# Down products in four passes over 16-byte granules, with the activations moved, in a one-core encoder layer

## Chip, core and metric

The kernel runs on one core of a Trainium2 chip. The metric is device time in microseconds (us) of one execution; the time before is the median of three runs. TensorE (PE) does the matmuls, and its weight loads are shown apart (PEld); VectorE (DVE), ScalarE (ACT) and GpSimd (POOL) work beside it, and SyncE (SP) issues the DMAs.

## The reference

One layer of a bidirectional encoder on 512 positions of width 1024, all in float32, with two half-step feed-forward blocks (FFN) around a mixing step:

```python
def swiglu(h, w_gate, w_up, w_down):
    return (jax.nn.silu(h @ w_gate) * (h @ w_up)) @ w_down
...
x = x + 0.5 * swiglu(rms_norm(x, ffn1_norm), ffn1_w_gate, ffn1_w_up, ffn1_w_down)
h = rms_norm(x, mix_norm)
u = h @ w_in
f_out = fourier_mixer(u[..., :o0], fnet_w, fnet_b)
a_out = gqa_attention(u[..., o0:o1], u[..., o1:o2], u[..., o2:], q_norm, k_norm)
x = x + jnp.concatenate([f_out, a_out], axis=-1) @ w_out
x = x + 0.5 * swiglu(rms_norm(x, ffn2_norm), ffn2_w_gate, ffn2_w_up, ffn2_w_down)
return rms_norm(x, final_norm)
```

The inner width of an FFN is 2752: 21 chunks of 128 and a tail of 64.

## The kernel before

**Operands in two parts.** Every float32 operand is split into a high and a low part that TensorE takes as `float32r`. A product is the sum of three matmuls: high weights with the high activation, high weights with the low one, low weights with the high one. `product` (lines 172 to 176) issues them, and these are the lines L173, L175 and L176 of the profile.

**An FFN.** `ffn` works through the chunks of the inner width in four groups (`GROUPS1`, `GROUPS2`). The first group's gate and up products run on the normalised input with all 512 positions. For the other groups `seven` computes gate and up of a chunk with seven products of half size instead of eight: line 407, where the moving operand is 256 columns of `rt` and the result goes to tiles named r, p and q. A chunk takes 84 of them: 7 products, 4 blocks of the input width, 3 parts. The second of a run of `seven` is cut into 64 and 192 columns (`parts_of`, `CUT`).

The activation of a chunk is put into a place of `at`: seven places, each 2 (high, low) x 512 columns. When a group is done, `down` multiplies its chunks with the down weights, for each of the eight blocks of 128 output channels (d), into a bank of PSUM `dn`: 512 columns, moving operand from `at`, weights from a slot of `ring`. The inner width's tail is two more matmuls per block, L487 and L488. `residual` (L528) then adds half of `dn` to x.

In the second FFN's last group the last three blocks (`LAST`) are done otherwise, in the stage `closing`: the first half of the positions in products of 256 columns (tiles `last`, with weights that begin `SKIP` elements into their slot), the second half by `by_tokens` (L519), where `at` is the weights and 384 columns of `tw` the moving operand. While the first group of an FFN runs, three places of `at` are lent as weight slots.

**Order.** In both FFNs TensorE's order is that of the code; the loads of weights and activations are put one step ahead by the loops (`prepare`, `PIECES`). The mixing stage between them follows a written order (`ORDER`); its matmuls are named mix in the profile. L998 to L1000 there have 256 columns from `ring`, L1057 256, 258 or 512 columns of `pos` and `both`, L1160 is a transpose.

**Places.** Tiles of a pool lie one behind another. `room` puts an unused tile between them, so many bytes of each partition. In the pool of the activations:

```python
room(ap, 192)
at = ap.tile([P, PLACES, 2, S], F32R, name=f"at{n_}")
room(ap, 192)
rt = ap.tile([P, 7, 2, KH, HALF], F32R, name=f"rt{n_}")
```

In the program that is built of it `at` begins at byte 119168 of a partition and `rt` at 148032; weights of the slots begin at 128 modulo 256, `at` at 128 and `rt` at 64.

Of the kernel before, what the change touches and what calls it, by code (L numbers as in the profile page):

```python
# [33 lines left out]
USES = "a11", "a12", "s1", "s2", "s4", "s3", "a22"  # L34
PIECES = (0, 2, 2, 0, 2, 1, 1)
KH = KD // 2
SKIP = 16
LAST = 3
CUT = 1, P // 2
HI_DVE = ("f0", "f1")  # L40
# [43 lines left out]
def encoder(ctx, tc, A, out):  # L84
    nc = tc.nc
# [6 lines left out]
    def room(pool, n):  # L92


        pool.tile([P, n // 4], F32, name=f"room{len(rooms)}")
        rooms.append(n)
# [6 lines left out]
    def bank(name):  # L103
        return pp.tile([P, S], F32, tag="bank", name=name)
# [40 lines left out]
    def raw_tile(src, name, n=KD):  # L145
        raw = wp.tile([P, KD, P], F32, tag="raw", name=f"raw_{name}")
        nc.sync.dma_start(out=raw[:, :n, :], in_=src)
        return raw
# [6 lines left out]
    def parts_of(n):  # L155

        return (slice(0, CUT[1]), slice(CUT[1], HALF)) if n == CUT[0] else (slice(0, HALF),)

    def weights(src, name, n=KD, raw=None, by_dma=False, skip=0):
        raw = raw or raw_tile(src, name, n)  # L160
        hi, lo = weight_slots(n, skip)
        if name in HI_DVE:
            nc.vector.tensor_copy(hi[:, :n, :], raw[:, :n, :])
        else:
            nc.scalar.copy(hi[:, :n, :], raw[:, :n, :])  # L165
        if by_dma:
            rest_by_dma(lo, hi, src)
        else:
            lows(lo[:, :n, :], raw[:, :n, :], hi[:, :n, :])
        return hi, lo  # L170

    def product(ps, whi, wlo, mhi, mlo, first, last, cut=False):
        nc.tensor.matmul(ps, whi, mhi, start=first, stop=False)  # L173
        for t in parts_of(CUT[0]) if cut else (slice(0, ps.shape[-1]),):
            nc.tensor.matmul(ps[:, t], whi, mlo[:, t], start=False, stop=False)  # L175
        nc.tensor.matmul(ps, wlo, mhi, start=False, stop=last)  # L176
# [92 lines left out]
    def ffn(norm, after, wgu, wd, wdt, groups, opening, closing):  # L269
# [4 lines left out]
        n_ = norm.n  # L274
        n_plain = len(groups[0])
        with tc.tile_pool(name=f"act{n_}", bufs=1) as ap, tc.tile_pool(name=f"sums{n_}", bufs=2) as sp:
            room(ap, 192)
            at = ap.tile([P, PLACES, 2, S], F32R, name=f"at{n_}")
            room(ap, 192)
            rt = ap.tile([P, 7, 2, KH, HALF], F32R, name=f"rt{n_}")  # L280
            wt, raws = [], {}
            free, where = list(range(PLACES)), {}
# [12 lines left out]
            def gate(c, between={}, by_dma=False):  # L295
                whi, wlo = weights(wgu[c], f"gu{n_}_{c}", by_dma=by_dma)
                ps = bank(f"gu{n_}_{c}")
                for k in range(KD):
                    between.get(k, int)()
                    product(ps, whi[:, k, :], wlo[:, k, :], hh[k], hl[k], k == 0, k == KD - 1)  # L300
                return ps
# [170 lines left out]
            def down(d, group, gi):  # L472

                js = [j for j in group if j != "t"]
                src, halves_ = wd[d][:, js[0] : js[-1] + 1, :], closing and gi == len(groups) - 1 and d >= KD - LAST
                raw = raws[d] = raw_tile(src, f"dn{n_}_{d}_{gi}", len(js))
                whi, wlo = weights(src, "", len(js), raw, skip=SKIP if halves_ else 0)
                if halves_:
                    token_weights(d, js)
                w = wt[d // 4][:, d % 4 * P : (d % 4 + 1) * P]  # L480

                def steps(ps, t):
                    for i, j in enumerate(group):
                        h, l = (at[:, where[j], o, t] for o in range(2))
                        first, last = i == 0, i == len(group) - 1
                        if j == "t":
                            nc.tensor.matmul(ps[:, t], w, h, start=first, stop=False)  # L487
                            nc.tensor.matmul(ps[:, t], w, l, start=False, stop=last)  # L488
                        else:
                            k = j - js[0]  # L490
                            cut = first and d == KD - LAST and t == slice(0, HALF)
                            product(ps[:, t], whi[:, k, :], wlo[:, k, :], h, l, first, last, cut)
                        yield

                return steps

            def token_weights(d, group):

                c = slice((d - KD + LAST) * P, (d - KD + LAST + 1) * P)
                hi, lo = (t[:, : len(group), c] for t in tw)  # L500
                raw = raws[d][:, : len(group)]
                nc.scalar.activation(hi, raw, AF.Copy, scale=0.5)
                nc.vector.scalar_tensor_tensor(
                    out=lo, in0=raw, scalar=0.5, in1=asf(hi), op0=ALU.mult, op1=ALU.subtract
                )
# [26 lines left out]
            every = slice(0, S)  # L532
            for gi, group in enumerate(groups):
                last = gi == len(groups) - 1
# [3 lines left out]
                else:  # L538
# [8 lines left out]
                    for i, c in enumerate(left):  # L547
# [6 lines left out]
                        while len(parts) * len(left) > (len(left) - 1 - i) * KH:  # L554
                            o = parts.pop(0)
# [14 lines left out]
                for d in range(KD):  # L570
# [8 lines left out]
                    ps = bank(f"dn{n_}_{d}_{gi}")  # L579
# [66 lines left out]
    cut = [0] + [4 * KD + k * S for k in (1, 2, 4, 6, 8)]  # L646
# [80 lines left out]
    with in_order():  # L727
        ffn(n0, n1, A["wgu1"], A["wd1"], A["wdt1"], GROUPS1, opening1, None)
# [3 lines left out]
    with tc.tile_pool(name="mix", bufs=1) as mp, tc.tile_pool(name="mixt", bufs=1) as mt:  # L732
# [69 lines left out]
        def project_ops(c, name):  # L802

            weight_ops(f"w{name}", A["wins"][c])

            def step(k):
                if k == 0:
                    banks[name] = bank_for(name, {"v": 1, "k": 3, "q0": 3}.get(name, 2))
                whi, wlo = ws[f"w{name}"]
                product(banks[name], whi[:, k, :], wlo[:, k, :], hh[k], hl[k], k == 0, k == KD - 1)  # L810

            for k in range(KD):
                op(f"{name}.{k}")(lambda k=k: step(k))
# [514 lines left out]
    first, rest = out[0].rearrange("p (k s) -> p k s", s=HALF), out[1].rearrange("p (c n) -> p c n", n=D)  # L1328
# [98 lines left out]
    with in_order():  # L1427
        ffn(n2, n3, A["wgu2"], A["wd2"], A["wdt2"], GROUPS2, lambda gate, column, row: [[gate(0, {KD - 1: column}), gate(1, {3: row})]], closing)
# [122 lines left out]
```

## Time and profile before

| | |
|---|---|
| time, median of 3 runs | 838.82 us (838.07 to 838.83) |
| span of the profiled execution, first to last instruction | 836.5 us |
| time of the runs beside the span | 2.3 us |
| PE busy | 829.6 us (99%) |
| DVE busy | 640.0 us (77%) |
| ACT busy | 465.3 us (56%) |
| DMA, mean | 107 GB/s |
| mean granted TensorE clock | 0.999 |

The time of the profiled execution itself wasn't recorded apart from its span; the 2.3 us are the difference between the median of the runs and the span. A group's row gives the busy time as a union of its instructions and the mean duration of one. Matmuls overlap, since each is shown until its result is out, so how fast TensorE goes is read from the distances between starts: in the timeline, or in the chain of work that ended last, where an instruction counts until the next begins.

### The profile page before, as it was taken

What the parts mean: (1) busy time and instruction counts of PE and PEld (TensorE: products, weight loads), DVE (VectorE), ACT (ScalarE), POOL (GpSimd) and SP (SyncE); (2) the same over time, 40 slices, a digit from 0 to 9 for tenths busy, and PEclk for the clock granted to TensorE, in tenths of its full rate; (3) what the DMA queues carried; (4) which work ended last, traced back from release to release, by engine and by line L of the source; (5) the groups of instructions that cost most, each with busy time, mean ns of one, the idle gap of its engine ahead of it and who ended that gap; (6) DMA issues with size and microseconds to landing.
All of it is one profiled execution on the core that took longest, in us unless ns stands there. A gap on an engine that the chain in (4) does not pass through costs nothing.

```text
span 836.5 us, 13664 instructions
## 1 busy us (share of the span) xinstructions
PE 829.6 (99%) x5406; PEld 751.5 (90%) x5406; DVE 640.0 (77%) x1005; ACT 465.3 (56%) x778; POOL 30.7 (4%) x34
## 2 busy tenths in 40 slices
PE   9999999999999999999999999999999999999997
PEld 6888998899989998888998888899988999899986
DVE  7898896489746947699998488999954896479573
ACT  7763664167524645677786356656622673257462
POOL 0110000000000000221100000100000000000001
PEclk9999999999999999999999999999999999999999
DMA  7664322323242213532020224443232332322222
GB/s 254 171 149 161 129 89 76 120 101 139 76 138 95 67 54 114 169 99 80 26 76 26 74 86 130 114 164 121 89 120 89 133 112 66 131 102 95 68 75 101
DMA packets 31168, 89.58 MB, mean 107 GB/s; under 512 B 3712, under 2 KB 8832, under 8 KB 31104
## 3 DMA queue, kind: packets, MB, share of 16 engines
q1 hardware_dynamic: 27776, 82.61, 29.0%
q0 software_dynamic: 2608, 5.12, 3.3%
q10 hardware_dynamic: 720, 0.98, 0.3%
q8 instruction: 42, 0.69, 0.3%
q14 instruction: 22, 0.18, 0.1%
HBM read 84.24 MB, written 2.10 MB: 103 GB/s over the span
## 4 chain that ended last, share of the span: by engine, by line
PE 98%; issue 0%; DMA 0%; DVE 0%; ACT 0%; POOLq 0%; POOL 0%; DVEq 0%
PE r L407 23%; PE q L407 11%; PE dn L175 9%; PE dn L173 9%; PE dn L176 9%; PE p L407 6%; PE mix L173 3%; PE mix L175 3%; PE mix L176 3%; PE gu L693 3%; PE gu L173 3%; PE gu L176 3%; PE gu L175 3%; PE mix L1203 2%; PE mix L1160 2%; PE mix L1134 1%
## 5 line engine op out<-in xcount | busy, mean ns | idle before, releaser
L407 PE MATMUL r<-rt,ring 128*128 128x256 f32 x1686 | 209.6, 276 | 0.0
L407 PEld LDWEIGHTS r<-rt,ring 128*128 128x128 f32 x1686 | 200.6, 188 | 0.9
L175 PE MATMUL dn<-at,ring 128*128 128x512 f32 x300 | 116.7, 389 | 0.0
L176 PE MATMUL dn<-at,ring 128*128 128x512 f32 x300 | 116.7, 389 | 0.0
L173 PE MATMUL dn<-at,ring 128*128 128x512 f32 x300 | 116.7, 389 | 0.0
L407 PE MATMUL q<-rt,ring 128*128 128x256 f32 x840 | 106.6, 276 | 0.0
L123 DVE TENSOR_TENSOR ring<-s,ring 128x1024 fp32r<-128x1024 f32 x70 | 85.5, 1221 | 24.1 <-ACT ring L366 20.8
L407 PEld LDWEIGHTS q<-rt,ring 128*128 128x128 f32 x840 | 100.4, 188 | 0.0
L528 DVE SCALAR_TENSOR_TENSOR gx<-dn,gx 128x512 f32<-128x512 f32 x61 | 41.9, 689 | 74.3 <-PE dn L176 74.3
L366 ACT CAST ring<-s 128x1024 fp32r<-128x1024 f32 x70 | 73.5, 1050 | 28.0 <-PE p L407 13.7
L165 ACT CAST ring<-raw_dn 128x768 fp32r<-128x768 f32 (+3 forms) x58 | 45.4, 786 | 76.7 <-PE dn L175 60.4
L176 PEld LDWEIGHTS dn<-at,ring 128*128 128x128 f32 x300 | 56.3, 188 | 11.8
L173 PEld LDWEIGHTS dn<-at,ring 128*128 128x128 f32 x300 | 56.3, 188 | 11.3
L175 PEld LDWEIGHTS dn<-at,ring 128*128 128x128 f32 x300 | 56.3, 188 | 11.2
L123 DVE TENSOR_TENSOR ring<-raw_dn,ring 128x768 fp32r<-128x768 f32 (+3 forms) x58 | 51.6, 892 | 5.9 <-PE r L407 4.6
L407 PE MATMUL p<-rt,ring 128*128 128x256 f32 x420 | 53.3, 276 | 0.0
L123 DVE TENSOR_TENSOR ring<-raw_g,ring 128x1024 fp32r<-128x1024 f32 x35 | 42.7, 1219 | 10.4 <-PE p L407 10.3
L407 PEld LDWEIGHTS p<-rt,ring 128*128 128x128 f32 x420 | 50.2, 188 | 0.0
L366 ACT CAST ring<-raw_g 128x1024 fp32r<-128x1024 f32 x35 | 36.8, 1053 | 13.9 <-DMA raw_g<-in_wgu 8.3
L415 ACT COPY p<-r 128x256 f32<-128x256 f32 x35 | 12.9, 370 | 49.1 <-PE r L407 48.7
L439 ACT ACTIVATE g<-g 128x512 f32<-128x512 f32 x35 | 22.2, 633 | 23.4 <-DVE g L438 23.1
L375 ACT CAST ring<-raw_u 128x512 fp32r<-128x512 f32 x35 | 21.8, 624 | 16.8 <-PE q L407 15.9
(318 smaller groups left out, 1557.1 us busy)
## 6 DMA issues: line engine op xcount, KB each, us to landing
raw_g<-in_wgu SPq DMA_DIRECT2D x35, 512.0 KB, 3.6
raw_u<-in_wgu SPq DMA_DIRECT2D x35, 512.0 KB, 4.3
raw_dn<-in_wd SPq DMA_DIRECT2D x40, 384.0 KB, 3.1
raw_gu<-in_wgu SPq DMA_DIRECT2D x12, 512.0 KB, 3.5
raw_o<-in_wo SPq DMA_DIRECT2D x8, 512.0 KB, 3.5
raw_dn<-in_wd SPq DMA_DIRECT2D x8, 448.0 KB, 3.3
raw_wq<-in_wins SPq DMA_DIRECT2D x4, 512.0 KB, 4.4
raw_f<-in_winf SPq DMA_DIRECT2D x4, 512.0 KB, 4.0
```

What stands on the lines that cost most here:

```text
L123: nc.vector.tensor_tensor(out=lo, in0=src, in1=asf(hi), op=ALU.subtract)
L165: nc.scalar.copy(hi[:, :n, :], raw[:, :n, :])
L173: nc.tensor.matmul(ps, whi, mhi, start=first, stop=False)
L175: nc.tensor.matmul(ps[:, t], whi, mlo[:, t], start=False, stop=False)
L176: nc.tensor.matmul(ps, wlo, mhi, start=False, stop=last)
L366: nc.scalar.copy(hi, src)
L375: nc.scalar.copy(hi, src)
L407: nc.tensor.matmul(ps[:, t], a[:, ks], b[:, i, t], start=first and i == 0 and o == 0, stop=i == KH - 1 and o == 2, skip_group_check=not first,
L439: nc.scalar.activation(b["g"], b["g"], AF.Silu)
L528: nc.vector.scalar_tensor_tensor(out=x[d][:, t], in0=ps[:, t], scalar=0.5, in1=x[d][:, t], op0=ALU.mult, op1=ALU.add)
L693: nc.tensor.matmul(pss[c], w[:, k % 2, c], m[k], start=k == 0 and m is hh and w is hi, stop=k == KD - 1 and w is lo,)
L1160: nc.tensor.transpose(pts[n][:, c * P : (c + 1) * P], prob[t, b, c][:, kc * P : (kc + 1) * P], ident)
```

## The change

A down product whose result covers all 512 positions reads its moving operand and writes its result through `turned`: 512 columns are seen as 32 x 4 x 4 and walked with the middle factor outermost. Four passes, each of 32 granules of 4 neighbouring elements (16 bytes), 64 bytes apart. Operand and result are walked alike, so that each element lands where it did. Both tail matmuls of a block do the same. The 256-column products of `closing`, and all other products, keep their order. The filler ahead of `at` goes from 192 to 144 bytes and that behind it from 192 to 240. `SKIP` goes from 16 to 4 elements.

```diff
-SKIP = 16
+SKIP = 4
...
-    def product(ps, whi, wlo, mhi, mlo, first, last, cut=False):
+    def turned(ap):
+        return ap.rearrange("p (a b c) -> p b a c", b=4, c=4)
+
+    def product(ps, whi, wlo, mhi, mlo, first, last, cut=False, turn=False):
+        if turn:
+            ps, mhi, mlo = turned(ps), turned(mhi), turned(mlo)
+            for a, b in ((whi, mhi), (whi, mlo), (wlo, mhi)):
+                nc.tensor.matmul(ps, a, b, start=first and b is mhi and a is whi, stop=last and a is wlo)
+            return
         nc.tensor.matmul(ps, whi, mhi, start=first, stop=False)
...
-            room(ap, 192)
+            room(ap, 144)
             at = ap.tile([P, PLACES, 2, S], F32R, name=f"at{n_}")
-            room(ap, 192)
+            room(ap, 240)
             rt = ap.tile([P, 7, 2, KH, HALF], F32R, name=f"rt{n_}")
...
+                        turn = t == every
                         if j == "t":
-                            nc.tensor.matmul(ps[:, t], w, h, start=first, stop=False)
-                            nc.tensor.matmul(ps[:, t], w, l, start=False, stop=last)
+                            o, h, l = (turned(p) if turn else p for p in (ps[:, t], h, l))
+                            nc.tensor.matmul(o, w, h, start=first, stop=False)
+                            nc.tensor.matmul(o, w, l, start=False, stop=last)
                         else:
                             k = j - js[0]
                             cut = first and d == KD - LAST and t == slice(0, HALF)
-                            product(ps[:, t], whi[:, k, :], wlo[:, k, :], h, l, first, last, cut)
+                            product(ps[:, t], whi[:, k, :], wlo[:, k, :], h, l, first, last, cut, turn)
```

In the program built of the changed kernel `at` begins at byte 119136 and `rt` at 148064.

## The prediction

> **What bounds the kernel now.** I read the page first: its busy times, its granted clock, its chain, its costliest groups.
>
> ```profile
> span 836.5 us, 13664 instructions
> PE 829.6 (99%) x5406; PEld 751.5 (90%) x5406; DVE 640.0 (77%) x1005; ACT 465.3 (56%) x778; POOL 30.7 (4%) x34
> PEclk9999999999999999999999999999999999999999
> PE 98%; issue 0%; DMA 0%; DVE 0%; ACT 0%; POOLq 0%; POOL 0%; DVEq 0%
> L407 PE MATMUL r<-rt,ring 128*128 128x256 f32 x1686 | 209.6, 276 | 0.0
> L175 PE MATMUL dn<-at,ring 128*128 128x512 f32 x300 | 116.7, 389 | 0.0
> L176 PE MATMUL dn<-at,ring 128*128 128x512 f32 x300 | 116.7, 389 | 0.0
> L173 PE MATMUL dn<-at,ring 128*128 128x512 f32 x300 | 116.7, 389 | 0.0
> L407 PE MATMUL q<-rt,ring 128*128 128x256 f32 x840 | 106.6, 276 | 0.0
> L407 PE MATMUL p<-rt,ring 128*128 128x256 f32 x420 | 53.3, 276 | 0.0
> ```
>
> TensorE is 98% of the chain that ended last, at full granted clock, with nothing idle before these groups. So the time is a count of matmuls times their spacing, and any change of spacing goes straight into the end. The mean durations (389, 276 ns) overlap and are no spacing; starts are. The timeline gives them for a run of down products:
>
> ```profile
> 131.65 0.39 PE L173 MATMUL dn<-at,ring 128*128 128x512 f32 x1
> ...
> 135.51 0.39 PE L176 MATMUL dn<-at,ring 128*128 128x512 f32 x1
> ```
>
> Eighteen rows, seventeen intervals: 3.86 / 17 = 227 ns for 512 columns. The chain, where matmuls follow without a gap, gives the other widths:
>
> ```profile
> 82.85 2.72 PE r L407 x24
> 436.71 1.44 PE mix L1057 x12
> 820.95 1.57 PE last L519 x9
> ```
>
> That is 113.3 ns (256 columns), 120 ns (258) and 174.4 ns (384). The points 258, 384 and 512 lie on a line: (227.1 - 120) / 254 = 0.422 ns a column, and 227.1 - 512 x 0.422 = 11 ns that doesn't grow with the columns. (For 384 the line says 173.1, the row 174.4.) What comes once per matmul, whatever its width, is its weight load:
>
> ```profile
> 131.88 0.40 PE L175 MATMUL dn<-at,ring 128*128 128x512 f32 x1
> 131.88 0.19 PEld L176 LDWEIGHTS dn<-at,ring 128*128 128x128 f32 x1
> ```
>
> The load for the next matmul (L176) starts with the running matmul (L175). I read the 11 ns as what this load costs the operand stream beside it. The stage of the r, p and q products has less of it: 113.3 - 256 x 0.422 = 5 ns. That this low state isn't given by the width shows in the mixing stage, where the same three lines run in two states:
>
> ```profile
> 425.03 0.11 PE mix L999
> ...
> 425.93 0.23 PE mix L1134
> ...
> 431.45 0.12 PE mix L998
> ...
> 432.75 0.12 PE mix L1000
> 432.87 0.23 PE mix L1134
> ```
>
> Eight products in 0.90 us are 113 ns each; twelve in 1.42 us are 118. Width and place are alike, and nothing idles inside either run; the state depends on how the stream fell in with its loads at entry.
>
> **What the change moves.** Instructions, their order and their operands' names are the same in both built programs on every engine; only three event-semaphore instructions of TensorE go. What differs is access patterns and addresses. 977 down products read and write in 4 passes of 32 granules: the nine hundred above and these rows:
>
> ```profile
> L487 PE MATMUL dn<-at,wt 128*128 128x512 f32 x16 | 6.2, 389 | 0.0
> L488 PE MATMUL dn<-at,wt 128*128 128x512 f32 x16 | 6.2, 389 | 0.0
> L173 PE MATMUL dn<-at 128*128 128x512 f32 x15 | 5.8, 389 | 0.0
> L175 PE MATMUL dn<-at 128*128 128x512 f32 x15 | 5.8, 389 | 0.0
> L176 PE MATMUL dn<-at 128*128 128x512 f32 x15 | 5.8, 389 | 0.0
> ```
>
> The addresses don't come out as the numbers in the diff say. The built program rounds each pool tile up to 32 bytes: the 144-byte filler takes 160, the 240-byte one 256. So `at` lies 32 bytes lower (119168 to 119136), not 48, and `rt`, which the second filler was to hold in place, lies 32 bytes higher (148032 to 148064). The 2946 products on `rt` (1686 + 840 + 420), at 113.3 ns 334 us of the span, are touched too. Their operand began 64 bytes before the weights modulo 256; now it is 32, so no longer a whole multiple of 64.
>
> **The rt products.** Only one place of the trace has 256 columns on an operand 32 bytes off a multiple of 64 against its weights: the four products of L1057 on the last part of `pos`.
>
> ```profile
> 446.96 0.40 PE L1057 MATMUL mix<-pos,eh 128*128 128x256 f32 x2
> 447.20 0.28 PE L1057 MATMUL mix<-pos,el 128*128 128x256 f32 x1
> 447.31 0.28 PE L1057 MATMUL mix<-pos,eh 128*128 128x256 f32 x1
> 447.43 0.27 PE L1160 MATMUL mix<-ident,e 128*128 128x128 f32 x1
> ```
>
> Four in 0.47 us: 117.5 ns. The run is short, so it may never have had time to fall into the 113 state; but 118 above is what this width costs outside it. I take 117.5: 4.2 x 2946 = **+12.3 us**. Bounds: 0, if the state holds at this distance, and 258 columns' 120 ns less two columns, 119.2, which is 5.9 x 2946 = +17.3 us. Below nothing I see no row: 113 is the least that this width shows.
>
> **The down products.** No row shows a granule-wise operand or result. The constant 11 ns is all that a better order against the weight load could take: 977 x 11.2 = -10.9 us at best. The nearest measured state of less collision is that of the rt products, with 5.4 ns left: 5.8 x 977 = **-5.7 us**, which I take. A load passes through all four granules of each 64 bytes, while a pass stays on one of them for 128 columns, so most of the load's reads fall elsewhere; but it must cross that one too, hence not the whole 11. The other bound is a loss: if the order makes load and stream meet twice as often, another 11.2 ns, +10.9 us; if every one of 128 granule breaks cost one column's time, 128 x 0.422 = 54 ns, +52.8 us.
>
> A page speaks against the patterns. The Trainium skill, "Advanced Engine Details and Errata", section PSUM Cachelines, says that any non-contiguous pattern in PSUM slows matmuls significantly, and also that pairs of neighbours should be contiguous for best throughput. Granules of four satisfy the second and break the first; no row here has such a pattern, and it is the third rival below.
>
> **The rest.** 62 half-width down products (`last`, in the closing) keep plain order, but weights move 48 bytes and `at` 32: 4.2 x 62 = +0.3 us, from 0 to 0.4. 42 products of L519 and 120 of the two openings only take weights from `at` 32 bytes lower; at 384 and 512 columns the constant is already the full one, so 0. VectorE and ScalarE write and read the moved tiles with the same instructions; their slack hides any small difference: VectorE is busy 65.6 of 90 us in such a stage,
>
> ```profile
> 165.00:255.00 90.00, 90.00 (x650) 84.34 (x649) 65.59 (x94) 44.54 (x74) 0.00 (x0) 1.00 0.31 106
> ```
>
> and if its 8 x 18 down products got shorter by the full 11 ns each, the stage would lose 1.6 us, far from making VectorE late. No DMA, no wait and no queue moves.
>
> **Sum.** +12.3 - 5.7 + 0.3 = +6.9 us on the profiled span: 836.5 to 843.4. The median of the runs is 838.8, 2.3 us beside the span; that stays: **845.7 us**.
>
> **Rivals.** *The low state holds, and the order helps* (other side): the rt products stay at 113.3, the down products shed 5.7 to 10.9 us: 827.9 to 833.1. For it: that state is found at two places of the code, L407 and L999, so it isn't bound to one tile. Against: the 117.5 rows, none of which is 113. It decides at a mean rt spacing under about 115.3 ns, where 2946 x 2.0 = 5.9 us eats the 5.7. Chance 0.19.
>
> *The order does nothing*: the down products stay at 227 because load and stream meet as often in granules; rt loses its state: 838.8 + 12.6 = 851.4. For it: the constant is equal at 384 and 512 columns and at various places of operands, as if no address mattered. Chance 0.14.
>
> *Granules cost*: down spacing rises above 227, by 11 ns (838.8 + 12.6 + 10.9 = 862.3) to 54 ns (904). For it: a pattern that the trace doesn't have at all, on both sides of the matmul. Against: a granule still holds four neighbours. Chance 0.27.
>
> *No address matters to TensorE at all*: both spacings stay, 838.8. The two states of the same lines at the same distance speak for something else than addresses. Chance 0.07. The Trainium skill, "TensorE: Matmul & The Clock Gate", Part 2, says that the load has a read port of its own and takes no read bandwidth from a running matmul. By that rule this would be the case; the constant of 11 ns and the two states speak against it, without refuting that they have another cause.
>
> **The numbers.** My forecast, rt lost and down products partly gained, has 0.33: from 836.2 (full gain, rt at 116: 838.8 + 8.0 + 0.3 - 10.9) to 856.4 (next to nothing gained, rt at 119.2). Range 828 to 872: all but the edge of the first rival (0.13 of 0.19), forecast, second and fourth whole, and half of the third: 0.80. A measurement of this kernel tells 0.2% (1.7 us) from no change. Faster by more: 0.19 and 0.04 from the forecast's low end, 0.23. Within: 0.07 and 0.03, 0.10. Slower: 0.67.
>
> **What would show it.** The chain's runs of 24 r products: 2.72 us before, 2.82 if the state is lost, 2.72 if not. The timeline's down products: 227 ns before, 221 by the forecast, 216 at best, 227 for nothing, 238 or more for granules. TensorE must stay 98% of the chain; if VectorE or a wait appears there, the sum itself is wrong. An `rt` spacing below 113.3 ns would overturn the bound I set at zero.

## The result, and the profile after

| | before | after |
|---|---|---|
| time, median | 838.52 us (838.07 to 838.83, 4 runs) | 853.16 us (853.14 to 853.22, 4 runs) |
| ratio | | 1.0175, 95% interval 1.0162 to 1.0189 |
| span of the profiled execution | 836.5 us | 851.3 us |
| granted TensorE clock | 0.999 | 0.999 |

The changed kernel is slower by 14.6 us, 14.8 us in the span. The page of the changed kernel, with the lines that answer to those shown of before:

```profile
span 851.3 us, 13667 instructions
PE 843.9 (99%) x5406; PEld 765.2 (90%) x5406; DVE 642.7 (75%) x1005; ACT 466.9 (55%) x778; POOL 30.7 (4%) x34
PE 98%; issue 0%; DMA 0%; DVE 0%; ACT 0%; POOLq 0%; POOL 0%; DVEq 0%
L415 PE MATMUL r<-rt,ring 128*128 128x256 f32 x1686 | 217.5, 281 | 0.0
L179 PE MATMUL dn<-at,ring 128*128 128x512 f32 x900 | 208.6, 387 | 0.0
L415 PE MATMUL q<-rt,ring 128*128 128x256 f32 x840 | 110.8, 281 | 0.0
L415 PE MATMUL p<-rt,ring 128*128 128x256 f32 x420 | 55.4, 281 | 0.0
```

TensorE is still 98% of the chain and its busy time rose by 14.3 us, so the time went into spacing. The groups say into whose. The r, q and p products of `rt`, whose code the diff doesn't touch, grew from 209.6 to 217.5, 106.6 to 110.8 and 53.3 to 55.4: 14.2 us together. The chain has the spacings:

```profile
83.27 2.84 PE r L415 x24
...
103.15 2.84 PE r L415 x24
...
139.90 28.58 PE dn L179 x126
```

Twenty-four r products took 2.72 us and take 2.84: 118.3 ns instead of 113.3. The 126 down products of this stretch, now in granules, take 28.58 / 126 = 226.8 ns. That is the 227 of before: the new order, with `at` where it now lies, did nothing to the time. The remaining half microsecond is mostly that of the 120 gate products whose weights lie in slots lent from `at`, now 32 bytes lower, while the operand that streams past them stays where it was. One of three like rows of 24 before, then the three after:

```profile
L173 PE MATMUL gu<-ring,at 128*128 128x512 f32 x24 | 9.3, 389 | 0.0
```

```profile
L181 PE MATMUL gu<-ring,at 128*128 128x512 f32 x24 | 9.5, 395 | 0.0
L183 PE MATMUL gu<-ring,at 128*128 128x512 f32 x24 | 9.5, 395 | 0.0
L184 PE MATMUL gu<-ring,at 128*128 128x512 f32 x24 | 9.5, 394 | 0.0
```

Their mean duration went from 389 to 394 and 395 ns, and the time from one start to the next grew by as much, 5 to 6 ns.

### The profile page after: what moved, and what is told of

It is laid out like the page before. It is cut to its first block, busy times and chain, and to the rows that moved or that the text cites. A ratio compares the mean times of both kernels' runs of the same rounds, so it can differ in the third digit from the quotient of the medians.

```text
span 851.3 us, 13667 instructions
## 1 busy us (share of the span) xinstructions
PE 843.9 (99%) x5406; PEld 765.2 (90%) x5406; DVE 642.7 (75%) x1005; ACT 466.9 (55%) x778; POOL 30.7 (4%) x34
## 4 chain that ended last, share of the span: by engine, by line
PE 98%; issue 0%; DMA 0%; DVE 0%; ACT 0%; POOLq 0%; POOL 0%; DVEq 0%
PE dn L179 25%; PE r L415 23%; PE q L415 12%; PE p L415 6%; PE mix L181 3%; PE mix L184 3%; PE mix L183 3%; PE gu L703 3%; PE gu L181 3%; PE gu L184 3%; PE gu L183 3%; PE mix L1213 2%; PE mix L1170 2%; PE mix L1144 1%; PE mix L1008 1%; PE mix L1009 1%
## 5 line engine op out<-in xcount | busy, mean ns | idle before, releaser
L415 PE MATMUL r<-rt,ring 128*128 128x256 f32 x1686 | 217.5, 281 | 0.0
L415 PEld LDWEIGHTS r<-rt,ring 128*128 128x128 f32 x1686 | 208.0, 188 | 1.0
L179 PE MATMUL dn<-at,ring 128*128 128x512 f32 x900 | 208.6, 387 | 0.0
L415 PE MATMUL q<-rt,ring 128*128 128x256 f32 x840 | 110.8, 281 | 0.0
L415 PEld LDWEIGHTS q<-rt,ring 128*128 128x128 f32 x840 | 104.3, 188 | 0.0
L415 PE MATMUL p<-rt,ring 128*128 128x256 f32 x420 | 55.4, 281 | 0.0
L374 ACT CAST ring<-raw_g 128x1024 fp32r<-128x1024 f32 x35 | 36.8, 1051 | 14.2 <-DMA raw_g<-in_wgu 7.6
L460 DVE TENSOR_TENSOR u<-g,u 128x512 f32<-128x512 f32 x35 | 24.0, 686 | 6.6 <-ACT u L459 6.6
L251 POOL TENSOR_TENSOR r<-ms,mhalf 128x4 f32<-128x4 f32 (+1 forms) x4 | 4.3, 1073 | 683.0 <-DVE ms L244 683.0
L459 ACT COPY u<-r 128x256 f32<-128x256 f32 x35 | 13.1, 374 | 28.0 <-PE r L415 28.0
L123 DVE TENSOR_TENSOR ring<-raw_u,ring 128x512 fp32r<-128x512 f32 x35 | 24.2, 690 | 5.4 <-PE r L415 2.9
```

Source lines behind the costliest of these rows:

```text
L123: nc.vector.tensor_tensor(out=lo, in0=src, in1=asf(hi), op=ALU.subtract)
L179: nc.tensor.matmul(ps, a, b, start=first and b is mhi and a is whi, stop=last and a is wlo)
L374: nc.scalar.copy(hi, src)
L415: nc.tensor.matmul(ps[:, t], a[:, ks], b[:, i, t], start=first and i == 0 and o == 0, stop=i == KH - 1 and o == 2, skip_group_check=not first,
L460: nc.vector.tensor_tensor(out=u, in0=b["g"], in1=u, op=ALU.mult)
```

## The experiments

Three theories stood: *placement* (rt lost its state because the second filler, rounded to 256 bytes, moved it by 32), *entry* (granule-wise down products ahead bring the stream into the rt products in another phase, wherever rt lies), and *distance* (the granule order pays, but only at the 48 bytes that were meant, not at the 32 that the rounding made of them). Below, "distance" is the start of the weights less the start of the operand that streams past them, in bytes modulo 256. Where one time is given, the kernel ran once, beside runs of before (838.69 us, or 838.50 as the median of 11 for the last four kernels).

### rt back at its place

`at` stays 32 bytes lower, `rt` returns to 148032, the half-width products have their distance of 64 again.

```diff
-            room(ap, 144)
+            room(ap, 160)
-            room(ap, 240)
+            room(ap, 224)
-SKIP = 4
+SKIP = 8
```

> The changed kernel with rt put back to 64 modulo 256 (at stays 32 bytes lower, granule order stays, weights of the half-width products 64 bytes off their operand again). Placement theory: the rt products lost their low state because rt moved by 32 bytes, and the granule order neither gains nor loses; then the r runs are 2.72 us for 24 again and the time is about 838.5 + 120 lent-slot gate products x 8 ns = 839.5 us. Entry theory: granule-wise down products ahead of the rt products bring the stream into them in another phase, whatever the address; then rt stays near 118 ns and the time near 853 us.

Measured: 838.73 us. The chain of this run:

```profile
83.34 2.72 PE r L415 x24
...
102.38 2.72 PE r L415 x24
...
614.32 28.54 PE dn L179 x126
```

The r runs are 2.72 us again, behind down products that are as granule-wise and as long (226.5 ns) as in the changed kernel. Placement holds; entry falls for this kernel.

The 256-column products of `closing` (tiles `last`, in plain order) say more. Against the changed kernel only their weights moved here, by 16 bytes (`SKIP`), and their operand in `at` stayed. The chain of the changed kernel, then of this one:

```profile
828.40 0.12 PE last L181
...
835.47 0.33 PE last L521 x3
```

```profile
814.23 0.12 PE last L181
...
821.04 0.33 PE last L521 x3
```

Sixty of them take 7.07 us (118 ns) at distance 48 and 6.81 us (113.5 ns) at 64. In every other kernel of this document `SKIP` keeps their weights 64 bytes beyond their operand, and the operand begins at eight different bytes modulo 256. The mean of all 62 stays at 114.0 to 114.5 ns there, against 118.1 in the changed kernel. So for these it is the distance that counts, and not where either operand lies.

### rt moved, and nothing else

The kernel before with 224 bytes in the second filler.

```diff
-            room(ap, 192)
+            room(ap, 224)
             rt = ap.tile([P, 7, 2, KH, HALF], F32R, name=f"rt{n_}")
```

> The kernel before with rt alone 32 bytes higher (filler behind the activations 224 instead of 192 bytes), nothing else changed. Placement theory: rt products at about 118.4 ns, 2934 x 5.0 = +14.7 us, 853.2 us; down products stay at 227 ns. Entry theory: rt stays at 113.3 and the time at 838.5 us.

Measured: 852.36 us, 13.7 us over before. The chain:

```profile
82.89 2.84 PE r L407 x24
88.57 1.42 PE q L407 x12
```

A filler of 32 bytes more, without any granule, makes 94% of the change's loss (13.7 of 14.6 us). (Expected were 14.7, from 5.0 ns for all 2934; against the span of before shown above, 836.5, this one's 850.5 is 14.0 more.) With `rt` the temporary tiles behind it move too, which VectorE, ScalarE and DMAs use; TensorE doesn't read them, and the down products of this run are where they were.

### The granule order, all places as before

```diff
-            room(ap, 144)
+            room(ap, 192)
-            room(ap, 240)
+            room(ap, 192)
-SKIP = 4
+SKIP = 16
```

> The granule order alone, all places as before (at 128, rt 64 modulo 256). Placement theory: rt at 113.3 ns, down products near 227 ns, 838.5 us. Entry theory: rt near 118, 853 us. Distance theory (the order pays only where operand and weights lie in different granules): down products at 227 or above, 838 to 845 us.

Measured: 844.94 us. That is the upper end of what the distance theory gave, but for another reason. The chain's rows:

```profile
122.33 2.83 PE r L415 x24
...
139.05 28.16 PE dn L179 x126
...
174.15 2.72 PE r L415 x24
...
616.02 28.55 PE dn L179 x126
...
651.74 2.83 PE r L415 x24
```

The down products have two spacings here, at the same addresses and in the same order: 28.16 / 126 = 223.5 ns in the first FFN, 3 ns under before, and 28.55 / 126 = 226.6 in the second, no gain. The loss is that of the rt products, which lie where they did: they run at 118 ns in their first stretch, at 113.3 in the second (from 174 us on) and third, and at 118 again throughout the second FFN. So entry isn't wrong, only not what happened in the changed kernel: at distance 64 rt's low state exists and can be missed. In the two kernels with rt at 32 (the changed one and the one above) no stretch reaches it.

The kernel before has a trace of this too. Its short r run between two stretches of down products,

```profile
135.90 1.41 PE r L407 x12
```

is at 117.5 ns, where the long ones are at 113.3. That it depends on what ran before is the nearest reading; no run varied that alone.

### The change as its numbers read

A true 48 bytes: `at` becomes a view that begins 16 bytes into a larger tile, and `rt` stays at its place.

```diff
-            room(ap, 144)
+            room(ap, 128)
-            at = ap.tile([P, PLACES, 2, S], F32R, name=f"at{n_}")
+            flat = ap.tile([P, PLACES * 2 * S + 8], F32R, name=f"at{n_}")
+            at = flat[:, 4 : 4 + PLACES * 2 * S].rearrange("p (a b c) -> p a b c", a=PLACES, b=2)
-            room(ap, 240)
+            room(ap, 224)
```

> The change as its numbers read: granule order with the activations truly 48 bytes lower (80 modulo 256, so one granule beyond the weights modulo 64), rt kept at 64. Placement theory without more: down products 227 ns, 838.5 to 839.5 us. Distance theory: the rounding spoilt the order, and at the true distance a down product takes 216 to 221 ns: 838.5 - 977 x 6 to 11 ns + 1 = 829 to 834 us.

Measured: 832.50 us, 6.2 us under before. Chain and group:

```profile
82.70 2.72 PE r L416 x24
...
610.45 27.72 PE dn L179 x126
...
694.06 3.96 PE dn L179 x18
```

27.72 / 126 = 220.0 ns, and 3.96 / 18 the same: a steady state 6.7 ns under the 227 of before, in both FFNs. 977 times 6.7 would be 6.5 us; 6.2 were gained, and not by all of them (see the better version below). The distance theory holds, with 6.7 ns where the prediction had 5.8, at the distance that the change was to have.

### The distance without the order

As above, but in plain order (`turn = False`).

```diff
-                        turn = t == every
+                        turn = False
```

> The true 48-byte distance without the granule order: activations at 80 modulo 256, down products in plain order, rt at 64. If the distance alone freed the down products, they would be near 220 ns and the time near 832.5 us. If it takes order and distance together (a plain stream passes through all granules and meets the load wherever it begins), they stay near 227 and the time at 838.5 to 839.5 us.

Measured: 854.36 us. Of the window from 139 to 175 us, the first and last of 124 down products in the chain:

```profile
138.83 0.23 PE dn L184
...
167.70 0.24 PE dn L184
167.94 1.52 PE r L416 x13
```

29.11 / 124 = 235 ns, worse than at distance 0 by 8; and of the 29 r runs of 24 that the chain lists, 19 are 2.83 us. I had expected no effect of the distance on a plain stream. Distance matters there too, and the gain at 48 needs order and distance together.

### 16 bytes higher, 16 bytes lower

Granule order; `at` at 144 and at 112 modulo 256 (distances 240 and 16), `rt` at its place, and `SKIP` 20 and 12, which keep the half-width products at 64. The edit of the first against the 48-byte version:

```diff
-            room(ap, 128)
+            room(ap, 192)
-            room(ap, 224)
+            room(ap, 160)
```

> Granule order with the activations 16 bytes higher than before (144 modulo 256, so 16 bytes beyond the weights; 80 is 16 beyond them only modulo 64). If the distance counts modulo 64, one granule ahead: down products 220 ns, 832 to 833 us, as with 48 bytes lower. If it counts by the line of 64 bytes or modulo 256, something else: 223 to 227 ns, 835 to 839 us.

> Granule order with the activations 16 bytes lower than before (112 modulo 256, 48 beyond the weights modulo 64). With this the four granule distances are complete: 0 (225 ns with the rt products in part disturbed), 16 (220), 32 (226.6). If only the granule just ahead is free: 224 to 227 ns, 836 to 845 us. If every odd distance is: 220 ns, 832.5 us.

Measured: 847.13 us and 851.50 us. Their chains, in this order:

```profile
617.74 28.71 PE dn L179 x126
```

```profile
621.24 29.03 PE dn L179 x126
```

227.9 and 230.4 ns, and in both the rt products miss their state in part, which is most of the time lost. Neither time was among those expected. Distance 240 equals 48 modulo 64 and has none of its gain: what counts isn't the granule alone.

### rt level with the weights

The kernel before with 256 bytes in the second filler: `rt` at 128, distance 0.

```diff
-            room(ap, 192)
+            room(ap, 256)
             rt = ap.tile([P, 7, 2, KH, HALF], F32R, name=f"rt{n_}")
```

> The kernel before with rt 64 bytes higher, at 128 modulo 256 and so level with the weights; nothing else. If rt needs a whole multiple of 64 bytes: 113.3 ns and 838.5 us. If the low state needs the distance of 64 itself: 117 to 120 ns, 849 to 858 us.

Measured: 857.46 us.

```profile
83.17 2.88 PE r L407 x24
...
93.25 2.88 PE r L407 x24
```

120.0 ns, steadily: a state of its own, 6.7 ns over the low one, as expected for the case that the distance of 64 itself is needed. A whole multiple of 64 is not what rt needs; of the three distances tried for it, 64 alone has the low state. I had named the multiple of 64 in the prediction as what rt loses; that was wrong, though the price came out near.

### Further distances for the granules

Granule order with `at` at 208, 48 and 64 modulo 256 (distances 176, 80, 64), made as above, with `SKIP` 36, 60 and 0.

> Granule order with the activations at 208 modulo 256: weights 176 bytes beyond them, 48 + 128. If the distance counts modulo 128 (two lines of 64 bytes): down products at 220 ns and 832.5 us, as at 48. If modulo 256: unlike 220, 223 to 235 ns and, with the rt products disturbed at entry, 838 to 853 us.

> Granule order with the weights 80 bytes beyond the activations. Measured so far, by distance modulo 128: 0: 225.0, 16: 230.2, 32: 226.6, 48: 220.3, 112: 227.7 ns. If 48 is the one low point: 223 to 230 ns, 838 to 851 us. If the low stretch goes on to 64 and 80, where the rt products have their own: 220 ns or less, 832.5 us or less.

> Granule order with the weights 64 bytes beyond the activations, the distance at which the rt products keep 113.3 ns. If that distance suits any order: 220 ns, 832 to 833 us. If the low state of the granule order belongs to 48 alone: 223 to 230 ns, 838 to 851 us.

Measured: 843.79, 836.20 and 839.03 us. The chains in this order:

```profile
618.05 28.96 PE dn L179 x126
```

```profile
612.80 28.16 PE dn L179 x126
```

```profile
614.53 28.56 PE dn L179 x126
```

229.8, 223.5 and 226.7 ns. Distance 176 is 48 + 128 and has no gain: the period is not 128. Distance 80 has half of it: 223.5 ns is the low end of what I had expected without a gain, and the time lies between my two expectations. All that was measured of granule-wise down products (stretches of 126, by distance; one kernel for each but 32 and 48):

| distance | 0 | 16 | 32 | 48 | 64 | 80 | 176 | 240 |
|---|---|---|---|---|---|---|---|---|
| ns each | 223.5 (first FFN), 226.6 (second) | 230.4 | 226.8, 226.5 | 220.0 | 226.7 | 223.5 | 229.8 | 227.9 |
| time, us | 844.9 | 851.5 | 853.2 (rt moved), 838.7 (rt back) | 832.5, 832.1 (below) | 839.0 | 836.2 | 843.8 | 847.1 |

### The better version

The 48-byte version had two blemishes: gate products and 45 down products with weights in lent slots, which moved with `at`, so that these down products were at distance 0. Here the lent slots (four places at first, as the edit shows, of which two are soon given back) begin 48 bytes further in. The larger tile is 32 bytes longer for it and the filler behind it as much shorter, so that `rt` stays.

```diff
-                    lent = [at[:, i].rearrange("p a b -> p (a b)") for i in range(PLACES - 4, PLACES)]
+                    lent = [flat[:, 16 + i * 2 * S : 16 + (i + 1) * 2 * S] for i in range(PLACES - 4, PLACES)]
```

> The true 48-byte version with the weight slots lent from the activations begun 48 bytes further in, so that weights lie at 128 modulo 256 everywhere again. The 120 gate products on lent slots were at 233.8 ns instead of 227 and 45 down products at 228.7 instead of 220; both back gives 120 x 6.8 + 45 x 8.7 ns = 1.2 us: 832.5 to 831.3 us, ratio to before 0.991. If the slots' overlap with the next place adds waits, 832 to 834 us.

Measured: 832.09 us against 838.50; ratio 0.9926, 95% interval 0.9913 to 0.9940. Groups of the 48-byte version, then of this one:

```profile
L179 PE MATMUL dn<-at 128*128 128x512 f32 x45 | 12.2, 390 | 0.0
L181 PE MATMUL gu<-ring,at 128*128 128x512 f32 x24 | 9.5, 396 | 0.0
```

```profile
L179 PE MATMUL dn<-at 128*128 128x512 f32 x45 | 11.8, 380 | 0.0
L181 PE MATMUL gu<-ring,at 128*128 128x512 f32 x24 | 9.3, 389 | 0.0
```

Both groups are lower, at 380 and 389 ns. For the down products only the weights moved, to distance 48. The span is 830.1 us against 830.7: half of the 1.2 us expected. Against the single run of the 48-byte version the difference in time (0.4 us) is within the spread of this one's runs (831.66 to 833.72), so only the step from before is shown: 6.4 us faster.

## Why the prediction was right or wrong

The direction and the range held, 853.16 in 828 to 872; the size didn't: +6.9 us forecast, +14.6 measured. It came near the second rival (order without effect, rt loses: 851.4), to which I gave 0.14. Of the 7.9 us by which the span missed the sum, 5.7 are the down term, 1.9 the rt term and 0.6 to 0.7 the lent slots; small groups took a few tenths back.

**What bounds the kernel** was right: TensorE stayed 98% of the chain, and each microsecond is found again in spacings times counts.

**The rounding of the pools** was right, and decided the case: the filler of 32 bytes alone costs 13.7 us.

**The rt term** was right in kind and short in size. +12.3 us were taken from the 117.5 ns of L1057; measured were 118.3, +14.2 us by the groups, inside its bounds (0 to 17.3). The reason given beside it was wrong: not a multiple of 64 is kept or lost, since distance 0 gives 120.0. That the row taken came within 1 ns was in part luck: `pos` lies at distance 224, not 32. That the low state also depends on entry, as the mixing stage suggested, was borne out, but at distance 64 only.

**The down term** is the step that failed: -5.7 us forecast, nothing measured (226.8 ns for 227). I took the low state of the rt products as the nearest row and assumed that it would be reached at any distance, because a pass that stays on one granule meets the load less often. The runs show that a low state exists for granules and has about the size (220.0 ns, 6.7 less) at distance 48, the one meant. Of the eight distances tried it is the only one with the whole gain. At 80, and at 0 in one FFN, half of it was there (223.5), and at 32, where the changed kernel was, nothing. My own text should have warned me: I had just argued that rt's state hangs on 32 bytes, and then let the down products' state hang on nothing.

**The constant of 11 ns** as a cost of the weight load beside the stream: supported, not settled. Moving only the operand, by 32 or 64 bytes, takes rt from 113.3 to 118.3 or 120.0. Moving only the weights, by 16 bytes, takes the half-width products from 118 to 113.5. With both moved and 64 bytes kept between them nothing changes. So the places of the two operands matter to each other. By what part of the memory, and whether other engines' traffic has a share, the runs don't show.

**The rule of the separate port** (the Trainium skill, "TensorE: Matmul & The Clock Gate", Part 2) would have left both spacings alone, as I read it in the fourth rival. The run with only rt moved contradicts that reading for float32r products: 852.36 us, with TensorE's own streams unchanged except in where one begins. Whether it is read bandwidth that the load takes was not measured, so the page's sentence itself is neither shown nor refuted.

**The rule on non-contiguous patterns in PSUM** (the Trainium skill, "Advanced Engine Details and Errata", PSUM Cachelines) doesn't bite for granules of four where both orders were run: at distance 0 they take 223.5 and 226.6 ns, plain order 227; at 48 they take 220.0, plain order 235. Its advice that pairs of neighbours should be contiguous is kept by all of these kernels, so no run tests it. The loss of 11 to 54 ns of the third rival, at 0.27, appeared nowhere: the worst distance has 230.4.

**The first rival** needed what the true 48 bytes had: rt's low state and a part of the 11 ns. It gave 827.9 to 833.1, and 832.5 was measured, but of another kernel than the one to be predicted.

**The rest** (half-width products, L519, lent slots) was put at +0.3 us. The lent slots cost 0.6 to 0.7 us of their own (120 products, 5 to 6 ns), which I had at 0, because 512 columns already showed the constant in full; the runs show that it can grow. The half-width products cost what was forecast (114.3 to 118.1 ns for 62 of them, 0.2 us).

## What to carry to other kernels

When TensorE is the whole chain, the spacing of matmuls is the first thing to read, and its constant part can depend on where operand and next weights lie against each other: move one operand by 16 and by 32 bytes, with all else kept, and read the spacing. Check in the built program that a filler moves what it is said to move, and nothing else; here a rounding moved the larger group by 32 bytes and the smaller one to a distance without gain. A gain found at one distance and one order belongs to the pair, and a neighbour that shares the allocation must be put back.

## What the runs showed of the hardware

A 512-column float32r product had steady spacings from 220.0 to 235 ns and a 256-column one of 113.3, 118 and 120.0 ns, at the same granted clock (0.998 to 1.0), by order and addresses and by something that neither accounts for: with places as before and only the down products turned, whole stretches of rt products ran at 118 or at 113.3 ns, and of down products at 223.5 or 226.6, from their start to their end. In plain order at distance 0, 512 columns take 226.7 ns (in stretches of 126) and 256 take 120.0; the lowest spacings, 220.0 and 113.3, both lie 6.7 ns under these. Why it is the same step was not tested. The distance counts beyond 128 bytes (48 gains 6.7 ns, 176 loses 3), and without any order that I can read from eight points; why 48 is the one is left open. So is what decides between two states at one distance. A distance that was run in one kernel only may have a second state that this kernel didn't meet.
